# Group norm of every second step four gaps later, and VectorE's share 3.0 in the two long gaps, in a chunked recurrence interleaved with the output product

## The chip, the cores and the metric

The kernel runs on one core of a Trainium2 chip. The metric is device time in microseconds (us), median of several runs. A core has five engines that run their own instruction streams in order and wait for each other by semaphores: TensorE (PE, with its weight loads as PEld), VectorE (DVE), ScalarE (ACT), GpSimd (POOL) and SyncE (SP, which issues DMAs here).

## The reference, cut to what matters

One layer over 2048 tokens of width 1024: an RMS norm, a product with `w_in`, three branches (spatial gating, convolution, and an RWKV-7 recurrence with 8 heads of 64), a product with `w_out`, an RMS norm with a residual, and a gated addition. The change touches the order of the recurrence's work alone:

```python
def step(state, inp):
    r_t, w_t, k_t, v_t, a_t, b_t = inp
    sa = jnp.einsum('bhvk,bhk->bhv', state, a_t)
    state = (state * w_t[:, :, None, :] + sa[..., None] * b_t[:, :, None, :]
             + v_t[..., None] * k_t[:, :, None, :])
    y_t = jnp.einsum('bhvk,bhk->bhv', state, r_t)
    return state, y_t
...
y = (y - mu_y) * lax.rsqrt(var_y + GN_EPS) * hvec(lnx_g) + hvec(lnx_b)   # mean, variance over each head's 64
y = y + jnp.sum(r * k * r_k.astype(f32), axis=-1, keepdims=True) * v
...
mix = jnp.concatenate([out_a, out_b, out_c], axis=-1) @ w_out[i]
```

## The kernel before, in words

**Three stages.** First the product with `w_in` and everything that is elementwise in it (to about 740 us), then the recurrence (755 to 1130 us), then the gate (to the end). The change is in the recurrence.

**The recurrence** takes the 2048 tokens in 32 chunks of 64, two to a step, so 16 steps, s = 0 to 15. In a chunk (`chain`) TensorE does a chain of small products: the first (L931) gives `rp`, VectorE copies it (L934), L943 multiplies it by a triangular inverse, L949 adds the state's part of the output, ScalarE copies the result (L952, L953), L961 makes the state's update and L966 the rest of the output. VectorE then adds the update to the state (L971) and writes two decayed halves (L976), which the next chunk's L931 reads.

**Gaps.** Between these products stand three gaps to a chunk, six to a step: after L931, after L949, after L966. A gap (`fill`) is a stretch of the program in which other work is put: what is due by a table (`forced`, then `late`, by the gap's number), eight or so products of the output projection (L1054, from a queue `fq`; `outgemm`), and VectorE's share of the inverse: `dve(DB[now[0] % 3] - spent[0])` takes instructions from a queue until the planned time that VectorE has in this gap, 3.4, 3.4 and 1.9 us, is used up. Work that is due counts against it (`use`). A long gap is one of the first two of a chunk.

**The inverse** serves two steps: 116 small multiplications and additions (L873, L878) after a transpose (L861) and a copy (L864), and at its end two transposes, L881 and L883. ScalarE copies the first one's result into place (L886, four copies). Then `below1` multiplies (L899, 64 tiny products on TensorE) what L883 and L886 have written; `below2` (L913) follows one gap later. Before it issues L899, `below1` empties the inverse's queue (`dve(1e9)`), so that what is left of the inverse comes into VectorE's stream there. It is due in the last gap of every odd step.

**The group norm.** `norm1(s)`: TensorE subtracts the mean (L991), ScalarE copies and squares (L995, L996), VectorE sums (L1001), ScalarE takes the root (L1002), VectorE inverts (L1004) and scales (L1005). `load_out(s)` loads what the output needs. `norm2(s)`: TensorE transposes (L1028), VectorE scales and adds (L1033, four times) and multiplies (L1035), ScalarE rounds (L1037), and one or two gaps later VectorE makes the remainder (L1041). `outgemm(s)` (L1054) starts eight gaps after the step's end.

**What sets the order.** TensorE's and VectorE's streams are in the order in which the program issues them; ScalarE's, GpSimd's and SyncE's come from a scheduler with priorities. All of it is fixed before the run. The numbers `n1`, `n2`, `n3` say how many gaps after a step's end its `norm1`, `norm2` and `outgemm` come: (3, 5, 8) for odd steps, (0, 4, 8) for even ones, (0, 2, 4) for the last three.

In what follows the four chunks of a pair of steps are called E0, E1 (the even step) and O0, O1 (the odd one).

Of the kernel before, what the change touches and what calls it, by code (L numbers as in the profile page):

```python
# [34 lines left out]
def hybrid_kernel(ctx, tc, x, x_t, w_in, vecs, wup, pw_w, sgu_wt, sgu_lnb, sgu_b,  # L35
# [23 lines left out]
    def new(tag, shape=(128, 1024), dt=F32):  # L59
        return sb.tile(list(shape), dt, tag=tag, bufs=BUFS[tag], name=nm(tag))  # L60

    def at(v):

        tc.cur_priority = int(v * 1000)
# [17 lines left out]
    def mps(shape=(128, 512), tag="m"):  # L82
        return psp.tile(list(shape), F32, tag=tag, bufs=2, name=nm(tag))
# [58 lines left out]
    def col(i):  # L142
        return vc[:, i:i + 1]
# [573 lines left out]
    forced = defaultdict(list)  # L717
    dq = deque()
    spent = [0.0]
    late = defaultdict(list)  # L720
    DB = (3.4, 3.4, 1.9)

    def use(t):

        spent[0] += t

    def dve(t):

        while dq and t > 0:
            try:  # L730
                c = next(dq[0])
                t -= c
                use(c)
            except StopIteration:
                dq.popleft()

    def mix(gens, budget=0.0):

        done = owed = 0.0
        for g in gens:  # L740
            for c in g:
                owed += MIX * c
                if owed > 0.4:
                    for c in pad(owed):
                        done += c
                        owed -= c
        for _ in pad(budget - done):
            pass

    def fill(budget):  # L750
# [4 lines left out]
        mix([g for w in (forced, late) for k in sorted(w) if k <= now[0] for g in w.pop(k)], budget)  # L755
        dve(DB[now[0] % 3] - spent[0])
        now[0] += 1

    def pad(t):

        f = now[0]
        while fq and t > 0 and fq[0][0] <= f:
            try:
                c = next(fq[0][1])
                fq[0][2] -= c
                t -= c
                yield c
            except StopIteration:
                fq.popleft()
# [7 lines left out]
    def load_chunk(u, s, i):  # L777

        if i == 0:
            u.update({"mk": [], "ar2": new("L", (128, 2, 4, 128)), "bk2": new("L", (128, 2, 4, 128))})  # L780
            u["ar"] = [u["ar2"][:, j] for j in range(2)]
            u["bk"] = [u["bk2"][:, j] for j in range(2)]
        c = 2 * s + i
        nc.sync.dma_start(out=u["ar"][i], in_=ar_s[c])
        nc.sync.dma_start(out=u["bk"][i], in_=bk_s[c].rearrange("p q k s -> p q (k s)"))
# [233 lines left out]
    def norm2(t):  # L1019


        while fq and fq[0][3] <= t - 2:
            for _ in pad(0.3):
                pass
        yn, (bs, oc) = F[t], F.pop(("o", t))
        yt = mps((128, 4, 128))
        for p in range(4):
            nc.tensor.transpose(yt[:, p, :], yn[:, p * 128:(p + 1) * 128], ident)  # L1028
        yield 0.43
        dve(0.4)  # L1030
        use(1.7)
        for p in range(4):
            nc.vector.scalar_tensor_tensor(out=oc[:, 4 + p, :], in0=yt[:, p, :], scalar=col(V_LG + p),  # L1033
                                           in1=bs[:, 0, p], op0=ALU.mult, op1=ALU.add)
        nc.vector.tensor_tensor(out=oc[:, 4:8, :], in0=oc[:, 4:8, :], in1=bs[:, 1], op=ALU.mult)  # L1035
        oT = [new("w", (128, 8, 128), F32R) for _ in range(2)]
        nc.scalar.copy(oT[0], oc)  # L1037

        def low():
            use(1.2)  # L1040
            nc.vector.tensor_tensor(out=oT[1], in0=oc, in1=oT[0], op=ALU.subtract)  # L1041

        late[now[0] + 1 + (now[0] % 6 == 4)].append(call(low))
        F[t] = oT
# [46 lines left out]
    def split_gate(k):  # L1091
        if k < 10:
            use(1.25)
            split(gw[k][0], gw[k][1], gw.pop(("r", k)))
# [85 lines left out]
    NS = 16  # L1180
# [5 lines left out]
    def call(fn, *a):  # L1186
        def g():
            fn(*a)
            return
            yield  # L1190
        return g()

    pg = []
    with tc.manual_schedule(engines={mybir.EngineType.PE}):
        at(P2)
        ring = new("ri", (128, 4, 256))
        state = ring[:, 2]
        nc.gpsimd.memset(state, 0.0)
        for s in range(4):
            for i in range(2):  # L1200
                load_chunk(U[s], s, i)
            if s == 0:
                load_v(U[0], 0)
        with tc.manual_schedule(engines={mybir.EngineType.DVE}):
            tl = tail()
            fq.append([0, tl, 48 * 0.216 * NT, -2])

            def go(t, *gens):
                at(P2)
                dve(0.5)  # L1210
                mix(gens, t)
                dve(t - 0.5)

            go(9.75)
            for s in range(2):
                for i in range(2):
                    go(2.1, scores(U[s], s, i, "c"))
            inverse(B[0])
            for s in range(2):
                for i in range(2):  # L1220
                    go(1.0, turn(U[s], i))
            for i in range(2):
                go(2.1, scores(U[2], 2, i, "c"))
                go(1.0, turn(U[2], i))
            go(12.0)
            go(1.7, below1(B[0]))
            go(1.1, below2(B[0]))
            for s in range(NS):
                f = now[0]
                at(P2 + 0.4 * f)  # L1230
                if s + 1 < NS:
                    forced[f + 2].append(call(load_v, U[s + 1], s + 1))

                even = s % 2 == 0
                if s + 3 < NS:
                    un = U[s + 3]
                    forced[f + (0 if even else 1)].append(scores(un, s + 3, 0))
                    forced[f + (1 if even else 3)].append(scores(un, s + 3, 1))
                    if even:
                        forced[f + 1].append(call(inverse, B[s // 2 + 1]))  # L1240
                    forced[f + 2].append(turn(un, 0))
                    forced[f + 5].append(turn(un, 1))
                if not even and s + 1 < NS:
                    forced[f + 5].append(below1(B[s // 2 + 1]))
                    forced[f + 6].append(below2(B[s // 2 + 1]))
                if s + 4 < NS:
                    un = U[s + 4]
                    forced[f + 3].append(call(load_chunk, un, s + 4, 0))
                    forced[f + 4].append(call(load_chunk, un, s + 4, 1))
                if s == NS - 2:  # L1250
                    for n, k in enumerate((8, 9, 10, 0, 1, 2, 3)):
                        forced[f + 1 + n].append(call(load_gate, k))
                        forced[f + 2 + n].append(call(split_gate, k))
                    forced[f + 8].append(call(gate_in, 0))
                    forced[f + 10].append(call(gate_x2, 0))
                    forced[f + 12].append(call(gate_tr, 0))
                yc = new("yc", (128, 4, 128))
                for i in range(2):
                    state = chain(s, U[s], i, state, yc)
                f = now[0]  # L1260

                n1, n2, n3 = (0, 2, 4) if s >= NS - 3 else (3, 5, 8) if s % 2 else (0, 4, 8)
                forced[f + n1].append(norm1(s, yc))
                forced[f + (1 if n2 == 2 else 2)].append(call(load_out, s))
                forced[f + n2].append(norm2(s))
                fq.append([f + n3, outgemm(s), 48 * 0.216, s])
                U[s].clear()
        P3 = P2 + 0.4 * now[0]
        gates = [gate_mm(0)]

        def upto(g):
            for c in g:
                if c is None:
                    return

        fill(BUD)
        while fq and fq[0][0] <= now[0] + 3:
            fill(BUD)
        now[0] += 1
        fill(0)  # L1280
        upto(gates[0])
        now[0] += 4
        while fq or forced or late:
            fill(BUD)
        for k in range(4, 8):
            load_gate(k)
            split_gate(k)
        for i in range(16):
            at(P3 + 1.4 * i)
            g = gates[0] if i == 0 else gate_mm(i)  # L1290
            for n, _ in enumerate(g):
                if n == 2 and i < 15:
                    gate_in(i + 1)
                    gate_x2(i + 1)
                if n == (18 if i == 0 else 36) and i < 15:
                    gate_tr(i + 1)
# [58 lines left out]
```

## Time and profile before

| what | us |
|---|---|
| median of 3 runs (lowest to highest) | 1432.69 (1430.08 to 1432.87) |
| the profiled execution's own time | 1433.92 |
| its span, first to last instruction | 1432.2 |
| TensorE busy | 1376.5 (96%) |
| VectorE busy | 1009.7 (71%) |
| ScalarE busy | 579.2 (40%) |
| GpSimd busy | 243.6 (17%) |

The profile is one execution. Its rows give the start, the duration and the engine of each instruction, with the idle time of that engine ahead of it in brackets and what ended it. Busy shares are an average over the three stages; in the recurrence the instructions themselves have to be followed. Products are pipelined on TensorE, so the time that a group takes is read from its start to the next one's start, and the printed duration is a little longer.

### The profile page before, as it was taken

Reading aid. Unit: us, or ns where it says so; the run is one execution under the profiler, and the core shown is the slowest. Engines: PE = TensorE matmul, PEld = TensorE weight load, DVE = VectorE, ACT = ScalarE, POOL = GpSimd, SP = SyncE. Lnnn points to the kernel's source line nnn. Section 1 sums busy time; section 2 is a strip of 40 time slices with the busy share of each in tenths; the row PEclk is TensorE's granted clock in tenths of the full one; section 3 lists DMA queues with packets and bytes.
Section 4 is the critical chain, followed back from the end, with each engine's and each line's share of the span. In section 5 each row is a group of like instructions: output and inputs, shape, how many; then the busy total and the mean of one; then the engine's idle time right before and its main releaser. Section 6 shows DMA issues by size and latency. Waiting matters only on the chain.

```text
span 1432.2 us, 24400 instructions
## 1 busy us (share of the span) xinstructions
PE 1376.5 (96%) x9701; PEld 1100.4 (77%) x9701; DVE 1009.7 (71%) x2003; ACT 579.2 (40%) x913; POOL 243.6 (17%) x284
## 2 busy tenths in 40 slices
PE   7998999999999999999899999999998989999998
PEld 6876877787898778778677777777776767888887
DVE  6599994885527999777666597789779544545453
ACT  6334445555332344444333554544553543111121
POOL 5431221221501000000111211211221101111120
PEclk9999999999999999999999899999999999999999
DMA  8432466679534458755822833242331534232331
GB/s 335 147 148 89 144 207 193 189 259 298 207 107 157 173 183 249 221 149 187 251 89 78 318 114 105 86 138 82 124 100 57 167 117 147 100 140 100 121 115 44
DMA packets 158311, 223.29 MB, mean 156 GB/s; under 512 B 58236, under 2 KB 108149, under 8 KB 158198
## 3 DMA queue, kind: packets, MB, share of 16 engines
q1 hardware_dynamic: 158066, 221.68, 47.1%
q8 instruction: 76, 1.25, 0.4%
q14 instruction: 37, 0.30, 0.1%
q10 hardware_dynamic: 132, 0.06, 0.0%
HBM read 132.58 MB, written 89.13 MB: 155 GB/s over the span
## 4 chain that ended last, share of the span: by engine, by line
PE 69%; DVE 24%; ACT 3%; issue 2%; DMA 2%; POOL 0%; ACTq 0%; POOLq 0%; DVEq 0%
PE z L300 32%; PE z L1167 12%; PE z L1054 6%; DVE inv L452 6%; PE c L1144 3%; DVE inv L873 3%; DVE inv L878 3%; PE z L312 2%; PE m L820 2%; PE m L240 1%; DVE mk L245 1%; DVE L L976 1%; DVE inv L861 1%; PE m L1123 1%; PE c L943 1%
## 5 line engine op out<-in xcount | busy, mean ns | idle before, releaser
L300 PE MATMUL z<-h,w 128*128 128x512 f32 x2592 | 631.6, 398 | 1.5 <-ACT zl L336 1.4
L300 PEld LDWEIGHTS z<-h,w 128*128 128x128 f32 x2592 | 485.0, 189 | 119.3 <-issue 6.0
L1054 PE MATMUL z<-h,w 128*128 128x512 f32 x768 | 203.5, 408 | 0.6 <-DVE w L1041 0.6
L452 DVE SCALAR_TENSOR_TENSOR inv<-inv,vc,inv 128x1024 f32<-128x1024 f32 x120 | 171.7, 1449 | 1.4
L1054 PEld LDWEIGHTS z<-h,w 128*128 128x128 f32 x768 | 138.4, 190 | 31.2 <-DVE w L1041 1.0
L283 POOL TENSOR_TENSOR w<-w,w 128x1024 fp32r<-128x1024 f32 x26 | 71.6, 2755 | 238.3 <-PE z L300 172.5
L1167 PE MATMUL z<-L,w 128*128 128x512 f32 (+1 forms) x384 | 96.3, 394 | 0.0
L1151 ACT ACTIVATE inv<-inv 128x512 f32<-128x512 f32 (+1 forms) x33 | 20.5, 620 | 182.1 <-DVE inv L1150 182.1
L1167 PE MATMUL z<-h,w 128*128 128x512 f32 (+1 forms) x384 | 93.1, 390 | 0.8 <-DVE inv L1150 0.8
L873 DVE TENSOR_TENSOR inv<-inv,inv 128x48 f32<-128x48 f32 (+23 forms) x464 | 85.7, 219 | 2.3
L878 DVE TENSOR_TENSOR inv<-inv,inv 128x48 f32<-128x48 f32 (+23 forms) x464 | 84.2, 217 | 1.2
L1167 PEld LDWEIGHTS z<-h,w 128*128 128x128 f32 x384 | 71.3, 188 | 17.4 <-DVE inv L1150 1.2
L1150 DVE TENSOR_TENSOR inv<-z,L 128x512 f32<-128x512 f32 (+1 forms) x32 | 21.8, 683 | 89.1 <-PE z L1167 89.1
L1167 PEld LDWEIGHTS z<-L,w 128*128 128x128 f32 x384 | 70.4, 188 | 15.3
L1111 POOL TENSOR_TENSOR inv<-inv,pg 128x1024 f32<-128x1024 f32 x16 | 38.3, 2397 | 218.0 <-DMA inv<-mx_s 168.1
L245 DVE RECIPROCAL mk<-mk 128x256 f32<-128x256 f32 x40 | 65.8, 1708 | 12.1 <-ACT mk L637 8.0
L825 DVE TENSOR_TENSOR mk<-m,mask 128x512 f32<-128x512 f32 x58 | 37.5, 683 | 35.9 <-PE m L820 31.7
L978 POOL TENSOR_TENSOR ri<-ri,pc 128x256 f32<-128x256 f32 x31 | 19.5, 629 | 236.1 <-DVE L L976 225.9
L312 PE MATMUL z<-w,h 128*128 128x256 f32 x384 | 52.5, 293 | 0.9 <-ACT h L262 0.9
L312 PEld LDWEIGHTS z<-w,h 128*128 128x128 f32 x384 | 50.3, 197 | 3.0 <-ACT h L262 1.6
L829 ACT COPY inv<-mk 32x128 f32<-32x128 f32 x128 | 37.8, 295 | 35.9 <-DVE mk L825 33.1
L282 ACT CAST w<-w 128x1024 fp32r<-128x1024 f32 x26 | 27.3, 1048 | 60.1 <-DMA w<-in_w_in_dram 44.4
(245 smaller groups left out, 1959.0 us busy)
## 6 DMA issues: line engine op xcount, KB each, us to landing
w_s<-w SPq DMA_DIRECT2D x58, 512.0 KB, 3.4
w<-w_s SPq DMA_DIRECT2D x58, 512.0 KB, 5.3
w<-in_w_in_dram SPq DMA_DIRECT2D x26, 512.0 KB, 3.8
L<-in_x_dram SPq DMA_DIRECT2D x16, 512.0 KB, 7.3
ar_s<-L SPq DMA_DIRECT2D x16, 512.0 KB, 4.7
wo_s<-w SPq DMA_DIRECT2D x16, 512.0 KB, 4.5
L<-ar_s SPq DMA_DIRECT2D x32, 256.0 KB, 3.1
L<-bk_s SPq DMA_DIRECT2D x32, 256.0 KB, 3.9
```

Of the source, the lines that this page charges most:

```text
L245: nc.vector.reciprocal(t[:, g * 256:(g + 1) * 256], t[:, g * 256:(g + 1) * 256])
L283: nc.gpsimd.tensor_tensor(out=ws[1], in0=wr, in1=ws[0], op=ALU.subtract)
L300: nc.tensor.matmul(z[:, g * 512:(g + 1) * 512], lhsT=ws[a][:, k * 128:(k + 1) * 128], rhs=h[:, b, k, :], start=(n == 0), stop=(n == 23))
L312: nc.tensor.matmul(z[:, i * 256:(i + 1) * 256], lhsT=h[:, b, k, i * 128:(i + 1) * 128], rhs=ws[k // 4][a][:, (k % 4) * 256:(k % 4 + 1) * 2 ...
L452: nc.vector.scalar_tensor_tensor(out=ac, in0=y[:, i:i + HT], scalar=col(V_CW + 2 * i + ct), in1=ac, op0=ALU.mult, op1=ALU.add)
L829: nc.scalar.copy(g["g"][32 * q:32 * q + 32, 0, 4 * ci:4 * ci + 4, :], mk[32 * q:32 * q + 32, par, :, s0:s0 + 32])
L873: nc.vector.tensor_tensor(out=tmp[:, o:o + n, :m], in0=tl[:, lo:hi, m:m + 1].to_broadcast([128, n, m]), in1=ml[:, m, :m].unsqueeze(1).to_b ...
L878: nc.vector.tensor_tensor(out=tl[:, lo:hi, :m], in0=tl[:, lo:hi, :m], in1=tmp[:, o:o + n, :m], op=ALU.add)
L1054: nc.tensor.matmul(mx[:, nh * 512:(nh + 1) * 512], lhsT=oT[a][:, k, :], rhs=wo[k // 4][:, b, k % 4, nh * 512:(nh + 1) * 512], start=(k == ...
L1111: nc.gpsimd.tensor_tensor(out=x2, in0=x2, in1=pg[0], op=ALU.mult)
L1144: nc.tensor.matmul(pp, lhsT=pT[:, a, k, :], rhs=gw[8 + k][b][:, nh * 512:(nh + 1) * 512], start=(n == 0), stop=(n == 5))
L1167: nc.tensor.matmul(z, lhsT=xT[a][:, k, :], rhs=gw[k][b][:, sl], start=(k == 0 and n == 0), stop=(k == 7 and n == 2))
```

## The change

Two tables change. The first two of VectorE's planned shares become 3.0 us. Of the even steps, all but 0 and 12 (and 14, which is among the last three) get (4, 5, 8) instead of (0, 4, 8): `norm1` four gaps later, `norm2` one gap later and in the table `late`, which is gone through after `forced`, so behind `below1`, which is due in the same gap; and `load_out` one gap later. These are steps 2, 4, 6, 8 and 10.

```diff
-    DB = (3.4, 3.4, 1.9)
+    DB = (3.0, 3.0, 1.9)
...
-                n1, n2, n3 = (0, 2, 4) if s >= NS - 3 else (3, 5, 8) if s % 2 else (0, 4, 8)
+                n1, n2, n3 = (0, 2, 4) if s >= NS - 3 else (3, 5, 8) if s % 2 else (0, 4, 8) if s in (0, NS - 4) else (4, 5, 8)
                 forced[f + n1].append(norm1(s, yc))
-                forced[f + (1 if n2 == 2 else 2)].append(call(load_out, s))
-                forced[f + n2].append(norm2(s))
+                forced[f + (1 if n2 == 2 else 3 if n1 == 4 else 2)].append(call(load_out, s))
+                (late if n1 == 4 else forced)[f + n2].append(norm2(s))
```

No instruction is added or taken away. On VectorE the inverse of a pair is dealt out otherwise. Of its 116 multiplications and additions, 15 stood in E0's last gap, 41 in E1's long gaps, 6 in E1's last, 27 in O0's long gaps, 15 in O0's last and 12 in O1's long gaps; now it is 11, 35, 6, 27, 15 and 22, and the copy L864 has moved from E0's long gaps to its last. The end of E1's long gaps, just ahead of the state's update, on VectorE before (names are tiles; the last two numbers of a row are the size, which shrinks as the inverse goes on):

```order
L878 TENSOR_TENSOR inv_7278<-inv_7278,inv_7666 128x4x18
L878 TENSOR_TENSOR inv_7278<-inv_7278,inv_7666 128x3x18
L873 TENSOR_TENSOR inv_7666<-inv_7278,inv_7667 128x4x17 x2
L878 TENSOR_TENSOR inv_7278<-inv_7278,inv_7666 128x4x17 x2
L873 TENSOR_TENSOR inv_7666<-inv_7278,inv_7667 128x4x16 x2
L878 TENSOR_TENSOR inv_7278<-inv_7278,inv_7666 128x4x16 x2
L971 TENSOR_TENSOR ri_4887<-c_7758,ri_4887 128x256
L976 TENSOR_TENSOR L_7722<-ri_4887,pc 64x256 x2
```

The same place now:

```order
L878 TENSOR_TENSOR inv_7258<-inv_7258,inv_7666 128x4x19
L878 TENSOR_TENSOR inv_7258<-inv_7258,inv_7666 128x3x19
L873 TENSOR_TENSOR inv_7666<-inv_7258,inv_7667 128x4x18
L873 TENSOR_TENSOR inv_7666<-inv_7258,inv_7667 128x3x18
L971 TENSOR_TENSOR ri_4887<-c_7754,ri_4887 128x256
L976 TENSOR_TENSOR L_7719<-ri_4887,pc 64x256 x2
```

The update has ten instructions of the inverse fewer ahead of it, counted from E0's update. The second place is the end of O1 on VectorE, from the inverse's last instructions to the next chunk's copy L934. Before:

```order
L878 TENSOR_TENSOR inv_7278<-inv_7278,inv_7666 128x8 x2
L881 STREAM_TRANSPOSE inv_7666<-inv_7278 128x32x16
L883 STREAM_TRANSPOSE inv_7278<-inv_7666 128x512
L1033 SCALAR_TENSOR_TENSOR w_8052<-m_8169,vc,w_8049 128x128 x4
L1035 TENSOR_TENSOR w_8052<-w_8052,w_8049 128x512
L971 TENSOR_TENSOR ri_4887<-c_8090,ri_4887 128x256
L976 TENSOR_TENSOR L_8054<-ri_4887,pc 64x256 x2
```

And now:

```order
L1001 TENSOR_REDUCE grs_8159<-yn_8144 128x8
L878 TENSOR_TENSOR inv_7258<-inv_7258,inv_7666 128x8 x2
L881 STREAM_TRANSPOSE inv_7666<-inv_7258 128x32x16
L1004 RECIPROCAL grs_8159<-grs_8159 128x8
L1005 TENSOR_TENSOR yn_8144<-yc_7554,grs_8159 128x512
L971 TENSOR_TENSOR ri_4887<-c_8062,ri_4887 128x256
L976 TENSOR_TENSOR L_8026<-ri_4887,pc 64x256 x2
L883 STREAM_TRANSPOSE inv_7258<-inv_7666 128x512
L1033 SCALAR_TENSOR_TENSOR w_8081<-m_8246,vc,w_8078 128x128 x4
L1035 TENSOR_TENSOR w_8081<-w_8081,w_8078 128x512
L934 COPY ri_4887<-c_8263 128x256
```

The sum L1001 of `norm1` now stands ahead of the inverse's end, and L883 behind the state's update. The third place is TensorE in O1, from the second long gap to the next chunk's L931. Before:

```order
L949 MATMUL c_8145<-L_6711,ri_4887 64x64 x8
L1028 MATMUL m_8169<-ident,yn_7934 128x128 x4
...
L961 MATMUL c_8090<-L_7722,L_6712 64x64 x8
L966 MATMUL c_8145<-mk_6937,L_7722 64x64 x8
L837 MATMUL m_8213<-ident,L_7799 128x128 x4
L899 MATMUL m_8219<-inv_7278,inv_7668 32x32 x32
```

And now, with five products L1054 between L899 and L1028 and three behind it (left out here):

```order
L949 MATMUL c_8122<-L_6688,ri_4887 64x64 x8
L991 MATMUL m_8145<-cen,yc_7554 128x128 x4
...
L961 MATMUL c_8062<-L_7719,L_6689 64x64 x8
L966 MATMUL c_8122<-mk_6937,L_7719 64x64 x8
L837 MATMUL m_8200<-ident,L_7795 128x128 x4
L899 MATMUL m_8206<-inv_7258,inv_7668 32x32 x32
...
L1028 MATMUL m_8246<-ident,yn_8144 128x128 x4
```

L991 has come here from O0's first gap and L1028 has gone behind L899, which itself has not moved; it reads the tile that L883 writes (`inv_7258` here, `inv_7278` before). On ScalarE L995 and L996 move with L991, and L1037 from ahead of L903 (the copy of L899's result) to behind it, right ahead of L917 (the copy of L913's).

## Rows read from the trace of the kernel before

**Rows 1.** TensorE's idle time in the recurrence (740 to 1140 us), by releaser: total, times, longest.

```profile
PE c L931 <- issue: 10.5, 10, 2.3
```

**Rows 2.** One pair of steps as a window: busy us (instructions) by engine, clock, DMA.

```profile
911.00:961.00 50.00, 47.76 (x647) 38.16 (x642) 41.50 (x164) 25.68 (x56) 10.24 (x22) 1.00 0.34 103
```

**Rows 3.** Timeline, TensorE, the same pair: start, duration, instruction, [idle before].

```profile
936.22 1.09 PE L931 MATMUL c<-L,mk 128*64 128x64 f32 x16 [1.32 <-issue]
...
937.24 1.16 PE L991 MATMUL m<-cen,yc 128*128 128x128 f32 x8
...
938.15 2.11 PE L1054 MATMUL z<-h,w 128*128 128x512 f32 x8
...
940.19 0.68 PE L943 MATMUL c<-ri,inv 64*64 64x64 f32 x16
...
948.79 1.09 PE L931 MATMUL c<-L,mk 128*64 128x64 f32 x16 [0.66 <-issue]
...
954.04 0.66 PE L1028 MATMUL m<-ident,yn 128*128 128x128 f32 x4
...
958.17 1.20 PE L899 MATMUL m<-inv,inv 32*32 32x32 f32 x64
...
961.36 0.69 PE L931 MATMUL c<-L,mk 128*64 128x64 f32 x16
```

**Rows 4.** Timeline, VectorE, the same pair.

```profile
928.48 0.68 DVE L1001 TENSOR_REDUCE grs<-yn 128x8 f32<-128x512 f32 x1
...
930.48 0.69 DVE L1005 TENSOR_TENSOR yn<-yc,grs 128x512 f32<-128x512 f32 x1
...
932.22 0.36 DVE L878 TENSOR_TENSOR inv<-inv,inv 128x84 f32<-128x84 f32 x2
...
932.50 0.35 DVE L873 TENSOR_TENSOR inv<-inv,inv 128x80 f32<-128x80 f32 x2
...
935.25 0.41 DVE L971 TENSOR_TENSOR ri<-c,ri 128x256 f32<-128x256 f32 x1
...
935.70 0.87 DVE L976 TENSOR_TENSOR L<-ri,pc 64x256 f32<-64x256 f32 x2
...
939.63 0.41 DVE L934 COPY ri<-c 128x256 f32<-128x256 f32 x1
...
954.27 1.13 DVE L881 STREAM_TRANSPOSE inv<-inv 128x512 f32<-128x512 f32 x1
...
955.44 0.71 DVE L883 STREAM_TRANSPOSE inv<-inv 128x512 f32<-128x512 f32 x1
...
958.41 1.07 DVE L976 TENSOR_TENSOR L<-ri,pc 64x256 f32<-64x256 f32 x2
```

**Rows 5.** Timeline, ScalarE, the same pair.

```profile
925.94 0.59 ACT L995 COPY yc<-m 128x512 f32<-128x512 f32 x1 [3.14 <-PE m L991]
...
926.56 0.63 ACT L996 ACTIVATE yn<-yc 128x512 f32<-128x512 f32 x1
...
955.44 2.50 ACT L886 COPY inv<-inv 32x512 f32<-32x512 f32 x4 [0.27 <-DVE inv L881]
...
963.28 1.18 ACT L917 COPY inv<-m 32x512 f32<-32x512 f32 x2 [2.06 <-PE m L913]
```

**Rows 6.** Timeline, GpSimd, the same pair.

```profile
956.65 2.11 POOL L858 COPY mk<-L 64x256 f32<-64x256 f32 x4
```

**Rows 7.** TensorE waits in the pair of steps 0 and 1, timeline.

```profile
779.93 1.04 PE L931 MATMUL c<-L,mk 128*64 128x64 f32 x16 [1.46 <-DVE L L976]
```

**Rows 8.** Windows after idle stretches: busy us by engine, then the granted clock.

```profile
1082.00:1083.00 1.00, 1.00 (x21) 1.00 (x23) 1.00 (x9) 0.61 (x1) 0.00 (x0) 0.59 0.00 0
...
1101.00:1105.00 4.00, 1.63 (x20) 1.10 (x19) 3.87 (x22) 0.00 (x0) 0.66 (x1) 1.00 0.00 0
```

**Rows 9.** Timeline, TensorE, in the first of these stretches.

```profile
1082.00 1.00 PE L943 MATMUL c<-ri,inv 64*64 64x64 f32 x16 [2.07 <-DVE ri L934]
...
1083.78 2.94 PE L1054 MATMUL z<-h,w 128*128 128x512 f32 x8
```

## The prediction, made before the changed kernel ran

> **What bounds the kernel now.** I read the waits of TensorE first, then the windows by pair of steps, then the timeline of one pair engine by engine. In a window of one pair TensorE is busy 47.8 of 50.0 us and VectorE 41.5 [rows 2]; the streams of TensorE and VectorE are in program order, so TensorE sets the time and the others count only where it waits for them. Over the recurrence it waits mostly ahead of L931, the first product of a chunk [rows 1]. The timeline shows where: in O0 for 1.32 us and in O1 for 0.66 [rows 3]. The releaser named is "issue", but VectorE's rows tell more: L971 and L976, which write what L931 reads, start at 935.25 and 935.70, right behind a row of the inverse's instructions that has no pause [rows 4], and L931 starts at 936.22, half a microsecond after the first half of L976 began. So the two long gaps hold more work for VectorE than their share of TensorE's time, and the state's update queues behind it. In E0, E1 and at the end of O1 TensorE does not wait.
>
> Two pieces to be weighed stand at the other end of the pair. L899 needs L883 and the four copies L886. Now L883 starts at 955.44 and ScalarE's copies run from 955.44 to 957.94 [rows 4, 5], and L899 starts at 958.17 [rows 3], just behind them. There is no reserve: what makes these two later stops TensorE, since everything behind L899 on it waits too.
>
> **The change part by part.**
>
> *The shares, 3.0 for 3.4.* Ten of the inverse's instructions leave the stretch between E0's update and E1's update. Two in a row take 0.28 us, from 932.22 to 932.50 [rows 4], so 1.4 us. L971 at 935.25 would come at about 933.9; L931 in O0 can then follow the products ahead of it at once, and its whole wait of 1.32 us [rows 3] goes. I take 1.3 in each of the four pairs from steps 4/5 to 10/11, which repeat alike, 5.2 in all. Three other pairs feel the shares too; the one row that I show of them has 1.46 [rows 7], the lower bound is nothing, and I take 0.8 each, 2.4. Sum **-7.6** (bounds -5.2 and -9.6).
>
> *norm1 away from O0.* L991 takes 0.91 us there, from 937.24 to 938.15 [rows 3], and the wait of 0.66 ahead of O1's L931 goes as VectorE's norm leaves these gaps. That would be 1.57. But not all of it comes out: L943 needs VectorE's copy L934, which starts 3.93 us after L976 (935.70 to 939.63) [rows 4], behind the other step's `norm2`. With L931 at its new time, 0.57 after L976 starts, L934 is done 3.8 us after L931, where L943 now starts 3.97 after it (936.22 to 940.19) [rows 3]. So 0.15 is won ahead of L943 and 0.66 behind it: 0.8 in each of the five pairs, **-4.0** (bounds -3.3 and -7.9).
>
> *norm1 into O1.* Here is the loss. O1's L931 stands at 948.79, L1028 5.25 us behind it [rows 3], and L991 takes that place. After it come, one behind the other: L991 itself, 1.16; L995 and L996, 0.62 (925.94 to 926.56) and 0.63 [rows 5]; then on VectorE L1001, 0.6 of its 0.68; two small instructions of the inverse, 0.2; L881, 1.17 (954.27 to 955.44); L1004 and L1005, 0.9, of which L1005 is 0.69; L971, 0.45; L976, 1.07; L883, 0.71 [rows 4]. With 0.1 for hand-overs the norm's sum starts 7.7 us after O1's L931 and L883 ends 12.8 after it. On VectorE the last instructions of the inverse wait for ScalarE in L1001, and L883 waits for the state's update. L899, now 9.38 after O1's L931 (948.79 to 958.17), starts at 12.9. From there the next chunk's L931 was 3.19 away (958.17 to 961.36) [rows 3], and L1028 lies between them now, half as many products as L991, so 0.45. The chunk takes 16.5 us where it took 12.57: 3.9 more. 0.9 of it is L991, and 3.0 is TensorE standing still at L899. The copies L886 would hold L899 until about 12.3 in any case (L881 ends at 9.7, and they take 2.50). Five pairs: **+19.5**. Bounds: 2.4 if VectorE, which has nothing to do for about 1.5 us ahead of L1001, gains all of that in some way, and 4.5 if GpSimd's copies run into L1005 and L976; so +12 and +22.5.
>
> What GpSimd does is moved with it: the start of its work for the next inverse hangs on the inverse's last addition, so its copies L858, 2.11 for four [rows 6], again lie beside L976, which takes 1.07 there and 0.87 where none runs [rows 4]. I have used 1.07. The Trainium skill (SBUF, State Buffer, section on who interferes with whom) says more: a VectorE instruction with two inputs in SBUF and a GpSimd instruction that reads SBUF shut each other out for the whole instruction. By that rule L1005 and both halves of L976 could each lose one copy, an estimate of up to 1.6 us for a pair and 8 in all, and the sum would be 8 higher; the row beside it shows 0.2 in place of 1.1 for the two halves, so the page's worst case is not what this trace has there.
>
> *norm2 behind below1.* L1033 now waits for L1028 in the middle of the last gap, and L1037 stands on ScalarE ahead of L917. L917 starts 1.92 us after E0's L931 (961.36 to 963.28) [rows 5], and the score products L820 behind it need the buffer that it empties. By the same chain (L1028 at 15.1 after O1's L931, then L1033 and L1035 of about 1.9, then L1037 of about 1) it starts some 2.4 after E0's L931, and L820 waits about half a microsecond. I take 0.5, **+2.5** (0 and +4). VectorE's copy L934 there comes later too, but several groups of products lie ahead of its reader L943, which hide it; without them it would cost up to 0.6. `load_out` one gap later costs nothing: `norm2` is still two gaps behind, several us, and nothing on SP's queue behind it is due sooner.
>
> *The clock.* Through the whole pair the granted clock is 1.00 of 2.4 GHz [rows 2]. Elsewhere an idle stretch of 2.07 us ahead of L943 was followed by the lower level (0.59 on average in that microsecond) and the next eight products took 2.94 [rows 8, 9] in place of 2.11 [rows 3]; but the longest wait of all, 2.3 [rows 1], inside the window 1101 to 1105, left the clock at 1.00 [rows 8]. The new stall is longer than both, and small products stand on either side of it. A fall costs 0.8 for a group of eight and about as much again for the groups around it, 1.5 as an estimate, less where it falls into the stall. I take 1.0 for each of the five stalls, and 1.5 back in steps 0/1 where the 1.46 shrinks [rows 7]: **+3.5** (-1.5 and +9).
>
> Sum: -7.6 - 4.0 + 19.5 + 2.5 + 3.5 = **+13.9 us**. Against the profiled execution (1433.92, with a span of 1432.2, the rest lying around it) that is 1447.8; the profiled one is 1.2 over the median of 1432.69, so I predict 1446.6.
>
> **The rivals.**
>
> (a) *The clock holds.* No stall is followed by the lower level, as behind the 2.3 us wait [rows 1, 8]. Then the sum is 10.4: 1443.
>
> (b) *The clock falls behind every stall and for longer*, since little but tiny products lies around it. For it speaks that the stall is longer than the stretch in front of rows 9; the price is 2 us a stall in place of 1.0 and nothing back in steps 0/1, 6.5 more: 1453.
>
> (c) *The other side: TensorE isn't held at L899.* This needs L883 and L886 to be done by 9.9 us after O1's L931, in place of 12.9. Then O1 pays L991 less L1028, 0.5 a pair, and the shares and the emptied gaps are kept: -7.6 - 4.0 + 2.5 - 1 = -10, 1422.6. It decides from the point where L1001's operand is there by 4.7 in place of 7.7. Against it stands the order itself: L881 is behind L1001, which is behind two ScalarE instructions, which are behind L991.
>
> (d) *The two halves cancel.* The stall is 1.5 shorter, since VectorE's idle time ahead of L1001 turns out to be used, there is no wait at L917 and the clock holds: -7.6 - 4.0 + 12 = +0.4, 1433. It is also what comes out if the shares alone bite and the loss is smaller than each of its rows says.
>
> **How the numbers follow.** Forecast 0.45, (a) 0.25, (b) 0.18, (c) 0.06, (d) 0.06. Predicted is the forecast's 1446.6. The range 1438 to 1453 takes in the forecast with its bounds, (a) with a smaller loss at L917 and L899, and most of (b); it leaves out (c) and (d). A measurement of this kernel tells about 0.2%, 2.9 us, from no change. Slower by more than that are the forecast, (a) and (b), 0.88; within it (d), 0.06; faster (c), 0.06.
>
> **What would show it.** In the changed profile: L931 in O0 and O1 without idle time ahead of it; O1 16 to 17 us long in steps 5, 7, 9 and 11, with TensorE idle for about 3 us ahead of L899 and VectorE named as releaser; VectorE idle for about 1.5 us ahead of L1001 in O1; the other three chunks together about 2 us shorter; PEclk below 1.00 around the end of O1 in most of the five pairs. The prediction is wrong if L899 starts within a microsecond of L837, and then (c) holds; it is wrong in size if the pairs of steps 4 to 11 do not each grow by 2 to 3 us.

## The result, and the profile after

The changed kernel takes 1446.11 us (median of 6 runs, 1443.49 to 1447.56) where the kernel before took 1431.71 in the same comparison (6 runs, 1430.08 to 1433.51): a ratio of 1.0099, 95% interval 1.0086 to 1.0112. It is slower by 14.4 us, and the prediction of 1446.6 holds. Its profiled execution took 1447.56, with a span of 1445.8. The ratios in this text leave out two executions with a lower mean clock (0.845 and 0.785), one of the kernel with shares of 2.4 (1516.0 us, the one of it that was profiled) and one of the kernel before (1615.74).

First the waits of TensorE in the recurrence (740 to 1160 us), by releaser: total, times, longest.

```profile
PE m L899 <- DVE inv L883: 14.6, 5, 2.9
PE c L943 <- DVE ri L934: 6.1, 7, 1.6
...
PE c L931 <- issue: 1.9, 1, 1.9
```

The wait of [rows 1] is all but gone, 10.5 us in ten places to 1.9 in one, and a new one has come: five stops of 2.9 us ahead of L899, one in each pair with a moved norm, all for L883. TensorE's timeline over one pair (start, duration, instruction, idle time before), to be held against [rows 3]:

```profile
928.61 0.69 PE L931 MATMUL c<-L,mk 128*64 128x64 f32 x16
...
939.29 0.76 PE L931 MATMUL c<-L,mk 128*64 128x64 f32 x16
...
942.86 0.68 PE L943 MATMUL c<-ri,inv 64*64 64x64 f32 x16 [0.74 <-DVE ri L934]
...
955.52 1.16 PE L991 MATMUL m<-cen,yc 128*128 128x128 f32 x8
...
963.13 1.88 PE L899 MATMUL m<-inv,inv 32*32 32x32 f32 x64 [2.92 <-DVE inv L883]
964.94 2.50 PE L1054 MATMUL z<-h,w 128*128 128x512 f32 x5
967.24 1.06 PE L1028 MATMUL m<-ident,yn 128*128 128x128 f32 x4
...
969.50 0.92 PE L931 MATMUL c<-L,mk 128*64 128x64 f32 x16
```

O1's L931 stands at 950.61. The four chunks of this pair, from one L931 to the next, were 13.13, 12.36, 12.57 and 12.57 us before; now they are 13.12, 10.68, 11.32 and 18.89. E1 and O0 have won 1.68 and 1.25, and O1 has lost 6.32. VectorE's timeline at the end of O1, where [rows 4] had L881 at 954.27:

```profile
958.24 0.69 DVE L1001 TENSOR_REDUCE grs<-yn 128x8 f32<-128x512 f32 x1 [1.14 <-ACT yn L996]
...
959.18 1.09 DVE L881 STREAM_TRANSPOSE inv<-inv 128x512 f32<-128x512 f32 x1
...
960.33 0.69 DVE L1005 TENSOR_TENSOR yn<-yc,grs 128x512 f32<-128x512 f32 x1
960.94 0.42 DVE L971 TENSOR_TENSOR ri<-c,ri 128x256 f32<-128x256 f32 x1
961.39 0.85 DVE L976 TENSOR_TENSOR L<-ri,pc 64x256 f32<-64x256 f32 x2
962.27 0.71 DVE L883 STREAM_TRANSPOSE inv<-inv 128x512 f32<-128x512 f32 x1
```

VectorE stands still for 1.14 us ahead of L1001, with the inverse's last two small instructions, L881 and L883 behind it in its stream. L883 ends at 962.98 and L899 starts 0.15 later. On ScalarE the copies L886 hang on L881 and end at 962.80, almost as late (L899 doesn't need them, as the next section shows):

```profile
960.30 2.50 ACT L886 COPY inv<-inv 32x512 f32<-32x512 f32 x4 [0.26 <-DVE grs L1004]
...
971.65 0.58 ACT L917 COPY inv<-m 32x512 f32<-32x512 f32 x1 [0.40 <-PE m L913]
```

GpSimd's copies L858 are over at 959.50, before L1005 and L976 start:

```profile
957.75 1.75 POOL L858 COPY mk<-L 64x256 f32<-64x256 f32 x4
```

Windows around the stop (busy us by engine with instructions, then the granted clock as a share of 2.4 GHz):

```profile
958.00:963.00 5.00, 2.21 (x39) 1.54 (x37) 4.58 (x10) 3.52 (x8) 1.94 (x5) 1.00 0.69 195
963.00:965.00 2.00, 1.87 (x65) 1.83 (x65) 0.00 (x0) 0.41 (x1) 0.00 (x0) 0.56 0.42 145
965.00:967.00 2.00, 2.00 (x6) 1.61 (x6) 0.00 (x0) 1.15 (x2) 0.00 (x0) 0.50 0.00 0
...
971.00:973.00 2.00, 2.00 (x44) 1.51 (x38) 0.00 (x0) 1.41 (x3) 0.00 (x0) 1.00 0.81 235
```

Just as TensorE resumes, its clock drops to the lower level, 1.2 GHz, and stays there until about 970. What stands between L899 and the next L931 takes 6.37 us (963.13 to 969.50). The same follows each of the five stops, from 0.5 us ahead of L899 to 1.9 behind its start, in three of them for a shorter stretch; before, the pair's clock was 1.00 throughout [rows 2].

### The profile page after: what moved, and what is told of

It reads as the page before. It is cut to its first block, busy times and chain, and to the rows that moved or that the text cites. A ratio compares the mean times of both kernels' runs of the same rounds, so it can differ in the third digit from the quotient of the medians.

```text
span 1445.8 us, 24396 instructions
## 1 busy us (share of the span) xinstructions
PE 1382.9 (96%) x9701; PEld 1104.9 (76%) x9701; DVE 1005.6 (70%) x2003; ACT 579.9 (40%) x913; POOL 244.1 (17%) x284
## 3 DMA queue, kind: packets, MB, share of 16 engines
q8 instruction: 76, 1.25, 0.4%
## 4 chain that ended last, share of the span: by engine, by line
PE 69%; DVE 23%; ACT 3%; issue 2%; DMA 2%; SPq 0%; ACTq 0%; DVEq 0%
PE z L300 32%; PE z L1167 12%; DVE inv L452 6%; PE z L1054 6%; PE c L1144 3%; PE z L312 3%; DVE inv L878 3%; DVE inv L873 3%; PE m L820 2%; PE m L240 1%; DVE mk L245 1%; DVE L L976 1%; PE m L1123 1%; DMA w<-in_gate_w_dram 1%; PE m L899 1%
## 5 line engine op out<-in xcount | busy, mean ns | idle before, releaser
L1054 PE MATMUL z<-h,w 128*128 128x512 f32 x768 | 212.4, 420 | 0.6 <-DVE w L1041 0.6
L1054 PEld LDWEIGHTS z<-h,w 128*128 128x128 f32 x768 | 142.1, 195 | 32.1 <-DVE w L1041 1.1
L857 POOL COPY inv<-mk 32x128 f32<-32x128 f32 x64 | 23.4, 366 | 164.5 <-DVE mk L825 162.8
```

Source lines behind the costliest of these rows:

```text
L1054: nc.tensor.matmul(mx[:, nh * 512:(nh + 1) * 512], lhsT=oT[a][:, k, :], rhs=wo[k // 4][:, b, k % 4, nh * 512:(nh + 1) * 512], start=(k == ...
```

## The experiments

All times are medians; each kernel was compared with runs of the kernel before on the same chip, at 1431.7 to 1433.0 us. Line numbers move by two or three where a kernel has lines added; the text names the line that it is in the changed kernel.

### Either half alone

Only the shares (3.0, with the norm where it was):

```diff
-    DB = (3.4, 3.4, 1.9)
+    DB = (3.0, 3.0, 1.9)
```

> The shares of 3.0 us alone; the norms stay where they were. Theory A (the norm's new place makes the stall at L899, the shares only gain): the waits ahead of L931 in O0 go, 1.3 to 1.7 us in each of the pairs 4/5 to 10/11 and up to 3 in 0/1, L899 starts where it did, and the kernel is 6 to 10 us faster than before, about 1423. Theory B (the smaller share pushes the inverse's end out, and the norm only has a part in where it lands): on VectorE L881 and L883 now stand behind L976 in O1, so L881 ends about 11.7 us after O1's L931, the copies L886 end at 14.2, L899 starts at 14.3 in place of 9.4, and the clock falls behind it; that is 4 to 5 us a pair in six pairs, about 1455.

Measured: 1446.05 us, ratio 1.0107 (1.0090 to 1.0125). The shares alone cost as much as the whole change, by theory B's mechanism but below its price. At the end of O1, whose L931 is at 951.37, VectorE, then TensorE and ScalarE:

```profile
958.14 1.12 DVE L1033 SCALAR_TENSOR_TENSOR w<-m,vc,w 128x128 f32<-128x128 f32 x4
...
961.16 0.85 DVE L976 TENSOR_TENSOR L<-ri,pc 64x256 f32<-64x256 f32 x2
...
962.33 1.05 DVE L881 STREAM_TRANSPOSE inv<-inv 128x512 f32<-128x512 f32 x1
963.42 0.71 DVE L883 STREAM_TRANSPOSE inv<-inv 128x512 f32<-128x512 f32 x1
```

```profile
964.18 1.92 PE L899 MATMUL m<-inv,inv 32*32 32x32 f32 x64 [3.36 <-DVE inv L883]
```

```profile
963.42 2.50 ACT L886 COPY inv<-inv 32x512 f32<-32x512 f32 x4 [1.47 <-DVE inv L881]
```

With the smaller shares the inverse isn't finished in O1's long gaps, and its rest comes where `below1` empties the queue: behind `norm2` (L1033, L1035) and behind the state's update. TensorE stops for 3.4 us, in each of five pairs, without any norm sum in O1.

These rows also correct the text ahead of the prediction, which had L899 wait for the copies L886. L899 starts at 964.18 while the copies run until 965.92; in the kernel's code it reads another part of the tile that they write. So it needs L883 alone, and starts 12.8 us after O1's L931 where theory B had 14.3.

Only the norm (the table of gaps as in the change, shares 3.4):

```diff
-    DB = (3.0, 3.0, 1.9)
+    DB = (3.4, 3.4, 1.9)
```

> The norm's new place alone, with shares of 3.4. Theory A: the stall of 2.9 us at L899 stays as it is with both changes, with the clock's fall, and without the shares' gain the kernel is slower than with both, 1450 or more. Theory B: with the larger share L881 and L883 stand ahead of L1001, so L899 does not wait for L883; ScalarE's copies L886 now stand ahead of L952 and delay L961 by about 1 us; O0's wait of 1.3 stays; O0 is 0.8 to 1.2 shorter and O1 1.0 to 1.6 longer; the kernel takes 1431 to 1437, and the clock stays at 1.00 through the steady pairs.

Measured: 1439.88, ratio 1.0060 (1.0045 to 1.0075), dearer than expected. Here L881 and L883 are done by 958.4, ahead of L1001 at 962.28, and L899 doesn't wait, as theory B had it. VectorE, TensorE and ScalarE:

```profile
957.69 0.71 DVE L883 STREAM_TRANSPOSE inv<-inv 128x512 f32<-128x512 f32 x1
```

```profile
960.63 1.01 PE L961 MATMUL c<-L,L 128*64 128x64 f32 x15 [0.52 <-ACT L L952]
...
962.69 1.20 PE L899 MATMUL m<-inv,inv 32*32 32x32 f32 x64
```

```profile
957.69 2.50 ACT L886 COPY inv<-inv 32x512 f32<-32x512 f32 x4 [0.36 <-DVE inv L881]
960.22 0.37 ACT L952 COPY L<-c 64x256 f32<-64x256 f32 x1
```

What it costs is something else: L886 stands on ScalarE ahead of L952, for which L961 waits 0.5, and L961 and L966 together take 0.4 longer. O1 takes 14.4, 1.9 more than before, 0.9 of it L991. E0 is 0.4 longer, O0 0.7 shorter, and E1 keeps its full length of 12.4, so the pair is 1.6 longer. The two halves cost 14.4 and 8.2 alone and 14.4 together, so they don't add. With shares of 3.0, L883 ends 12.4 to 12.8 us after O1's L931 with the norm moved or not, and the stop is there once either way.

### The inverse's end ahead of the norm's sum

Both changes, but `norm1` of the moved steps empties the inverse's queue before it issues L1001 (`end` is true for these steps):

```diff
-        dve(0.5)
+        dve(1e9 if end else 0.5)
```

> Both changes, but norm1 of the moved steps empties the inverse's queue ahead of its sum L1001, so that L881 and L883 stand ahead of it. If the order L1001, L881, L883 is what stops TensorE (both theories, and the forecast's rival c), L899 waits under 0.6 us, the clock holds in the steady pairs, a steady pair takes 48.5 to 49.5 us in place of 50.6 before, and the kernel takes 1420 to 1426. If the stall comes from ScalarE's copies L886, which stand behind L996 now, L899 still waits 1.5 us or more, and the kernel takes 1435 or more.

Measured: 1426.91, ratio 0.9964 (0.9951 to 0.9976), faster than the changed kernel and the kernel before, and 0.9 above what was expected. VectorE and TensorE:

```profile
948.96 1.15 DVE L881 STREAM_TRANSPOSE inv<-inv 128x512 f32<-128x512 f32 x1
950.14 0.71 DVE L883 STREAM_TRANSPOSE inv<-inv 128x512 f32<-128x512 f32 x1
950.77 0.65 DVE L1001 TENSOR_REDUCE grs<-yn 128x8 f32<-128x512 f32 x1
952.99 0.20 DVE L1004 RECIPROCAL grs<-grs 128x8 f32<-128x8 f32 x1 [1.57 <-ACT grs L1002]
```

```profile
951.65 1.20 PE L899 MATMUL m<-inv,inv 32*32 32x32 f32 x64
```

L899 stands 9.55 us after O1's L931, against 12.52 in the changed kernel, and 3.68 ahead of the next, against 6.37. VectorE still waits, 1.57 us ahead of L1004 in place of 1.14 ahead of L1001, but L881 and L883 are no longer behind the wait. New small waits are what is left of the loss: 1.0 to 1.2 ahead of L1028 in three pairs, 0.7 ahead of L820 for L917 in five.

### The inverse emptied earlier, with the norm where it was

Shares 3.0, the old table, and the queue emptied in O1's second long gap:

```diff
+                    if 3 <= s < NS - 4:
+                        forced[f + 4].append(call(dve, 1e9))
                     forced[f + 5].append(below1(B[s // 2 + 1]))
```

> Shares 3.0 with the old places of the norm, and the rest of the inverse (L881 and L883 with it) emptied in O1's second gap of the five pairs, ahead of the wait for L943's operands. Theory B (it is the smaller shares that leave L881 and L883 until the state's update, and the norm's place matters little): no wait at L899, the clock stays at 1.00 in the five pairs, O0 still near 11.8 as in the shares alone, pair near 49.5 to 50; 1424 to 1430 us. Theory A (the norm in O1 was what stopped TensorE, and what the inverse-first kernel won it won by the norm's new place): the wait goes too, but the time stays at 1431 or above, since O0 keeps L991 and its wait. The difference to the kernel with both changes and the inverse first (1426.9) is what the norm's new place is worth.

Measured: 1438.06, ratio 1.0032 (1.0019 to 1.0046); neither text had it. VectorE and TensorE at the end of O1:

```profile
954.67 1.11 DVE L1033 SCALAR_TENSOR_TENSOR w<-m,vc,w 128x128 f32<-128x128 f32 x4
955.81 0.69 DVE L1035 TENSOR_TENSOR w<-w,w 128x512 f32<-128x512 f32 x1
...
957.77 1.05 DVE L881 STREAM_TRANSPOSE inv<-inv 128x512 f32<-128x512 f32 x1
958.86 0.71 DVE L883 STREAM_TRANSPOSE inv<-inv 128x512 f32<-128x512 f32 x1
```

```profile
959.63 1.92 PE L899 MATMUL m<-inv,inv 32*32 32x32 f32 x64 [2.29 <-DVE inv L883]
```

`norm2` of the even step is due in the same gap and comes first, 1.75 us, and VectorE has no pause in the whole gap; L899 still waits 2.3, and the clock falls behind each such stop. With the norm moved as well, the time falls by about 10 us (from 5.3 above the kernel before to 4.8 below it); there `norm2` is out of O1's last long gap, and the inverse is done in time. How much of the 10 us is the norm's own is not shown: no run empties the queue ahead of `norm2` with the norm left where it was, which might end the stop too.

### The clock, without the stop's cause touched

The changed kernel with twelve products of 128 x 512 ahead of L899 in the five pairs. They need nothing that is late, and L899 overwrites their result:

```diff
+        for _ in range(warm):
+            nc.tensor.matmul(zp.rearrange("p c t -> p (c t)"), lhsT=wo[0][:, 0, 0, 0:128], rhs=wo[0][:, 0, 0, 0:512],
+                             start=True, stop=True)
...
-                    forced[f + 5].append(below1(B[s // 2 + 1]))
+                    forced[f + 5].append(below1(B[s // 2 + 1], 12 if 3 <= s < NS - 4 else 0))
```

> The changed kernel with twelve products of 128x512 (about 3.1 us, results overwritten by L899's own) put ahead of L899 in the five stalls, so that TensorE works while it would stand still. L899 cannot start sooner; what can change is the clock alone. If TensorE's idle time is what brings the lower level, the level stays at 1.00 behind L899, and 8 to 10 us come back: 1436 to 1438. If the fall has another cause (the tiny products L899 and L913), it stays and the kernel takes 1446 to 1448.

Measured: 1432.93, ratio 1.0012 (1.0000 to 1.0024), 13.2 below the changed kernel and further down than expected. TensorE (L902 is the changed kernel's L899, L934 its L931, and O1's is at 946.49), then the window of the group behind:

```profile
955.86 3.00 PE L897 MATMUL m<-h 128*128 128x512 f32 x12
958.94 1.20 PE L902 MATMUL m<-inv,inv 32*32 32x32 f32 x64
...
962.55 0.69 PE L934 MATMUL c<-L,mk 128*64 128x64 f32 x16
```

```profile
960.00:965.00 5.00, 5.00 (x105) 4.09 (x98) 2.15 (x6) 2.28 (x4) 0.00 (x0) 1.00 0.03 7
```

L899 starts 12.45 us after O1's L931, as late as in the changed kernel, but the level stays at 1.00 and the next L931 follows after 3.61. Over the five stops the time from L899 to the next L931 is 28.2 us in the changed kernel and 18.1 here: 10.1 us are the clock's. Steps 12/13 add little: the end of O1 is 2.4 shorter there, but the level falls elsewhere in the same pair, E1 is 1.5 longer, and the pair is 0.9 shorter.

### Work that has to be done anyway, put into the stop

The changed kernel with `below1` behind L1028 and behind the products that followed it:

```diff
+        if first:
+            yield from pad(1.7)
...
-                    forced[f + 5].append(below1(B[s // 2 + 1]))
+                    (late if 3 <= s < NS - 4 else forced)[f + 5].append(below1(B[s // 2 + 1], 3 <= s < NS - 4))
```

> The changed kernel, with L899 and what hangs on it behind L1028 and the pieces of eight products that stand after L899 in the changed kernel, so that the 2.9 us are filled with work that has to be done anyway; VectorE's order is nearly unchanged. If TensorE's standing still is what costs (14.6 us in five stalls) and the clock about 13 with it: L899 starts without a wait and the level stays at 1.00, and the time falls by 14 to 22 us from 1446, to 1424 to 1432. If what comes late is L883 for the whole pair, TensorE waits for the copies behind L899 instead (L913 or E0's L820 and L943), and the time is 1436 to 1446.

Measured: 1441.46, ratio 1.0057 (1.0037 to 1.0077). The level stays at 1.00 behind L899 in the five pairs and L899 has no wait, but only 5.7 us come back (8.7 above the kernel before, in place of 14.4), a time that the second expectation covers. TensorE's waits (L933, L945, L1030 are L931, L943, L1028):

```profile
PE c L933 <- issue: 11.1, 10, 1.9
PE c L945 <- DVE ri L936: 8.3, 8, 2.0
PE m L1030 <- DVE yn L1007: 4.7, 5, 1.0
```

The products are only taken from the gaps behind; there, in E0 and E1, VectorE's work is as late as before and TensorE now waits for it ahead of L931 (1.51 ahead of E1's). So the wait moves in good part. That VectorE's lost time is the whole cause is not shown: the kernel with the twelve useless products loses the same time on VectorE and is 8.5 us faster than this one. One difference seen is that L899 starts 14.85 us after O1's L931 here and 12.45 there, and what hangs on it comes later.

### How small a share

With the inverse's end first, shares of 2.7, then 2.4:

```diff
-    DB = (3.0, 3.0, 1.9)
+    DB = (2.7, 2.7, 1.9)
```

> Both changes with the inverse's end ahead of L1001, but shares of 2.7. More of the inverse is put off to the emptying in O1's second gap. If the wait ahead of L931 in E1 and O0 is already gone at 3.0, nothing is won there and the norm's sum and L1005 come later by the put-off instructions (some eight a pair, 1.1 us): L1028 waits for L1005 longer (1.0 to 1.2 with 3.0, about 2.2 here), 5 us over the five pairs; 1430 to 1434. If the gaps still held too much, another 1 to 3 us less than 1426.9.

> As with shares of 2.7 (1419.3), but 2.4. L943's wait for L934 in O0 (0.76 with 3.0, 0.41 with 2.7) shrinks by another 0.3; the put-off part of the inverse (about six instructions, 0.9 us) goes in front of L1001 and L1005, and L1028 waits that much longer, 1.4. Net +0.6 in each of five pairs; the pair of steps 12 and 13, where the step from 3.0 to 2.7 won 4.1, wins at most 1 more. 1420 to 1424. If the whole emptying fits in VectorE's idle time, 1417.

Measured: 1419.31 with 2.7, ratio 0.9896 (0.9875 to 0.9917), and 1436.26 with 2.4, ratio 1.0022 (1.0012 to 1.0032). Both expectations were missed, on opposite sides. TensorE's waits with 2.7:

```profile
PE c L943 <- DVE ri L934: 5.0, 7, 2.0
PE m L820 <- ACT inv L917: 3.7, 6, 0.7
PE m L1028 <- DVE yn L1005: 2.6, 5, 0.6
```

There is next to no wait ahead of L899 (under 0.1): L883 ends 9.5 us after O1's L931, 0.7 later than with 3.0, and that is just in time. L1028 waits 0.5 in each of four pairs, where with 3.0 it waited 1.0 to 1.2 in three; the fifth wait counted above lies in the last steps. Some 4 of the 7.6 us are in steps 12/13, 53.4 to 49.3, where with 3.0 L931 still waited 1.9 and the clock fell once more; the term for smaller shares had been thought spent.

`norm2` of the moved steps one gap later as well (6 for 5), with shares of 2.7 and of 2.4:

```diff
-else (4, 5, 8)
+else (4, 6, 8)
```

> Shares 2.7, the inverse's end first (1419.3 without what follows), and norm2 of the moved steps one gap later, behind L917 and the first score products. Theory: the prediction's term for norm2 behind below1 is real where nothing else stands in the way: there L1028 waits 0.5 for L1005 and L820 0.7 for L917, which stands behind L1037, in each of five pairs. Both waits go; 1.2 in a pair, 6.0 in all; 1412 to 1415. Rival: VectorE's L1033 and L1035 (1.8) now stand ahead of the second pair of L825 and of L971 in E0, and the update of E0 comes late by that; then L931 in E1 or L943 waits for it, and the time stays at 1417 to 1422.

> Both: shares 2.4 and norm2 one gap later. L1028 has no wait left to lengthen, so the smaller share costs less: by the first theory 1410 to 1415, not above the kernel with 2.7 and norm2 later by more than 1. By the rival (VectorE's order in E0 decides) 1418 to 1424.

Measured: 1418.49, ratio 0.9899 (0.9883 to 0.9916), no different from 1419.31; and 1451.09, ratio 1.0118 (1.0099 to 1.0137). In the first, the waits at L820 and L1028 shrink from 3.7 and 2.6 to 0.9 and 0.6, as the first theory had it, and come back at L943 (8.3 in place of 5.0) and ahead of E0's L931. The time is the rival's, though the place is only half its own:

```profile
PE c L931 <- ACT inv L903: 2.8, 5, 0.6
```

In the second, VectorE and TensorE at the end of O1, whose L931 is at 953.05:

```profile
963.58 1.04 DVE L881 STREAM_TRANSPOSE inv<-inv 128x512 f32<-128x512 f32 x1
964.66 0.71 DVE L883 STREAM_TRANSPOSE inv<-inv 128x512 f32<-128x512 f32 x1
```

```profile
965.52 1.61 PE L899 MATMUL m<-inv,inv 32*32 32x32 f32 x64 [2.94 <-DVE inv L883]
```

Neither text had this. VectorE's stream has no pause there from 946 to 966: the inverse no longer fits, L883 ends 12.3 us after O1's L931, and the 2.9 us stop and the lower clock are back, now without L1001 ahead of it. TensorE in steps 0/1 of the same kernel:

```profile
807.42 1.92 PE L899 MATMUL m<-inv,inv 32*32 32x32 f32 x64 [4.20 <-DVE inv L883]
```

This pair has no moved norm, and it takes 52.93 us where the kernel with 2.7 and `norm2` a gap later has 48.31. Its order doesn't hang on `norm2`'s place, so the kernel with 2.4 alone should pay these 4.6 us too; what makes up the rest of its 1436.26 stays open.

## Why the prediction was right, point by point

The pair shown grew from 50.63 to 54.01, +3.38; the terms for such a pair were -1.3, -0.8, +3.9, +0.5 and +1.0, +3.3.

- **The shares.** Ahead of O0's L931 the wait of 1.32 is gone, and E1 is 1.68 shorter where 1.3 was taken. In steps 0/1 the pair is 3.0 shorter, clock included, where 2.3 were put down. The sign of the term as a cause was wrong, though: see below.
- **norm1 away from O0.** The new wait ahead of L943 was forecast from L934's distance and is there, 0.74. O0 gained 1.25 where 0.8 was taken.
- **norm1 into O1.** L899 was to start 12.9 us after O1's L931 and starts 12.52 after it. VectorE's pause ahead of L1001 is 1.14 where about 1.5 was expected, and the releaser is the one named. L976 takes 0.85 and not 1.07, with GpSimd's L858 over at 959.5, before it. So the rule of the Trainium skill (SBUF, State Buffer, section on who interferes with whom) that would have added up to 8 us found nothing to act on in this place.
- **norm2 behind below1.** L917 starts 2.15 us after E0's L931, in place of 1.92, and L820 behind the five stops waits once, 0.2: next to nothing where 2.5 was taken. The mechanism exists, 0.7 a pair, once the stop is gone (the kernels with the inverse first).
- **The clock** was the mis-sized term: 1.0 was taken for each stop, and 1.5 to 2.75 was measured, 10 us in all. Rival (b)'s price, 2 us a stop, is what they cost on average; that steps 0/1 would give nothing back was its error. The shares' and O0's larger gains and the missing wait at L917 made up for it. The errors cancel in the sum; that it came within 0.5 us is luck.
- **The copies L886.** They were taken as a second bound on L899, 12.3 us, and "no reserve" was read from them. L899 doesn't need them. Before, L883 ended at 956.15 and L899 started at 958.17, right behind the products ahead of it, so 2.0 us were in hand. The sum doesn't change, since 12.9 was the later of the two.
- **The signs.** The stop, its releaser, VectorE's pause and the clock are as named. The sizes are off: O1 was to be 16 to 17 us long and is 17.6 to 18.9, the other three chunks were to be 2 us shorter together and are 2.9, and the pairs of steps 4 to 11 were to grow by 2 to 3 us each, while two of the four grew by 3.6 and 3.4.
- **Rival (c).** The inverse's end ahead of L1001 meets its condition (L899 at 9.55), and that kernel takes 1426.91 where (c) had 1422.6. (c) left out the waits at L820 and L1028, and its last term, -1, has no row.

By pairs the whole is -3.0, +2.5, +3.6, +3.4, +2.4, +2.3 and +0.3, +11.5 us. The recurrence also began 1.6 later in this profile (756.64 to 755.04). Other kernels, with the same work ahead of it, began anywhere from 755.1 to 756.5, so it need not be the change's; 0.5 is spread behind.

**The step that failed** is the split of the sum. The prediction gave all of O1's loss, 19.5 us, to the norm and counted the shares as a gain of 7.6. The runs show the reverse: the shares alone bring the stop, +14.4, and the norm alone doesn't, +8.2 for other reasons. The chain that it added up is right for the two together, but it took L881 behind L1001 as the norm's doing. It stands there because 22 of the inverse's instructions, in place of 12, are left for O1, which the change section's counts showed, and because something that waits or takes long, L1001 or `norm2`, stands ahead of it there. With the same 22 and nothing ahead of them, L883 ends 8.75 us after O1's L931 and L899 doesn't wait. A sum made term by term should have priced those ten where they went, and not only where they left. Rival (d)'s second reading, that the shares alone bite and little is lost, is refuted by the same run.

## What to carry to other kernels

Work that is taken out of one stretch of an in-order stream has to be priced where it lands, above all when the last piece of it is what another engine waits for: here ten small instructions put off made the end of a chain late, with the norm moved or not. Before a wait is put into a full stream, empty what others are waiting for ahead of it; that one change turned +14.4 us into -4.8, and smaller shares on top of it into -13.5, up to the point where the put-off work no longer fits. Filling a stop with other work shows what part of it is the clock's and what part is real lateness, which moves with the work.

## What was not expected of the hardware

Behind all five stops of 2.9 us ahead of L899 the clock went to the lower level, and behind the five of 2.3 us in the kernel with the inverse emptied earlier and the norm left where it was as well, although TensorE was busy without a break just before and after; the 2.3 us wait of [rows 8] had left it at 1.00. Where twelve large products filled the stop, it never fell there. The fall takes 1.5 to 2.75 us a time, half to nearly all of what the stop itself took, 10.1 us in all of the 13.2 us between the two kernels.
